# One block kernel on one core: the low half of every fourth weight unit of the SSD stage made by an accumulating load

## The chip, the cores and the metric

The kernel runs on one core of a Trainium2 chip. Its time is the device time of that core in microseconds (us): 2100.75 us, the median of 3 runs (2100.36 to 2102.08). Everything said of the inside of the kernel comes from one profiled execution, which took 2101.31 us; the profile's span, from the first to the last instruction, is 2099.6 us.

The engines are called by the profile's names: PE (matrix multiply) with PEld (its weight loads), DVE (VectorE), ACT (ScalarE), POOL (GpSimd) and SP (SyncE, which here only issues transfers).

## The reference

One residual block over 256 tokens of width 2048, in float32. The input is normalised (RMSNorm), multiplied by one large matrix, and its columns feed two token mixers: a stick-breaking attention of 16 heads, and a Mamba-2 SSD (64 heads of 64, 8 groups, chunks). Both are projected, gated, added, projected again and normalised; then a gated MLP with a short convolution follows. The part that the change touches is the projection into the SSD mixer and the mixer itself:

```python
proj = h @ w_in[i]
q, k, v, z, xbc, dt, g_sb, g_ssd = jnp.split(proj, cuts, axis=-1)
xbc = jax.nn.silu(causal_dwconv(xbc, ssd_conv_w[i], ssd_conv_b[i]))
xs, bm, cm = jnp.split(xbc, [SSD_INNER, SSD_INNER + SSD_GROUPS * SSD_STATE], axis=-1)
y = ssd_scan(xh, dt, a, bm, cm)
y = (y + xh * d_skip[i][:, None]).reshape(b, s, SSD_INNER) * jax.nn.silu(z)
y = rms_norm(y.reshape(b, s, SSD_GROUPS, SSD_INNER // SSD_GROUPS), ...)
```

Every product with a weight matrix has to come out with more than the precision of one pass of the matrix engine in its fast format (`fp32r`).

## The kernel before, in words

**Units.** All weights are cut on the host into 714 units of 128 x 1024 float32 (512 KB), in the order in which PE uses them. Each unit goes through three steps. SP loads it into `raw` (`load`, L74 to L79). ACT casts it to `fp32r` into `whi`, the high half (L63). DVE subtracts, `wlo = raw - whi`, which gives the low half (L64). L63 and L64 stand in the helper `split`, which `prep` calls (L81 to L95). PE then multiplies with both halves. `raw` has 5 buffers (`RBUFS`) and `whi` and `wlo` have 5 each (`WBUFS`).

**How far ahead.** `unit()` (L97 to L104) gives out the next unit's halves, and before that runs `prep` up to the unit three further on. With five buffers, the cast of unit v can start when PE has finished unit v - 5.

**Products.** `feat_mm` (L115, lines L112 and L113) makes 128 output features for all 256 tokens. It uses two units, and from each unit eight blocks of 128 x 128 as the stationary operand, first of `whi`, then of `wlo`. `tok_mm` (L136, lines L145 to L147) makes 512 features for 128 tokens at a time. It uses eight units for 2048 rows, and there the weights are the moving operand; each unit takes 12 matmuls.

**The SSD stage.** After eight joint units (0 to 7), the loop over the 8 groups uses units 8 to 161. A group is 4 feature tiles `ps_xs` (8 units), one `ps_bc` for B and one for C (2 units each), then `ps_z` (8 units): 20 units. The first group has only 14, since three of its `ps_xs` tiles come from the joint units. I number the units of a group 0 to 19: `ps_xs` has 0 to 7, `ps_bc` 8 to 11, `ps_z` 12 to 19.

**The work between.** The group's scan, `ssd_work` (L324 to L382), is a generator; `pump()` (L155) runs its next piece inside `ps_z` and the following `ps_xs`, after every fourth k step of `tok_mm` and after each feature tile. Its pieces follow each other through the engines: PE transposes the features (L332), DVE makes `xw` (L333) and `mm` (L338), POOL does three multiplications (L335, L336) and two masks (L339), ACT takes the exponential of `mm` (L347) and copies `pcb` (L345), then PE makes `po` (L353). Later DVE writes `csb` (L357), POOL adds it (L358), and PE makes `pd` (L363). POOL also issues two loads for each group: `csb<-gain` (L356, 256 KB) and the next group's `csb<-cs_dram` (L429, 1 MB).

**Order.** Each engine executes its own instructions in a fixed order. This order is not the order of the source: a planner in the framework writes it, and takes at each point an instruction whose operands are ready by its own reckoning, earlier source first. Across engines, semaphores enforce the dependencies. An instruction that waits holds up what stands behind it on the same engine, and this is so for transfers that POOL or SP issue as well. In the first part of the kernel and in two short stretches (`manual_schedule`), ACT and DVE keep the source's order.

Of the kernel before, what the change touches and what calls it, by code (L numbers as in the profile page):

```python
# [12 lines left out]
AF = mybir.ActivationFunctionType  # L13
ALU = mybir.AluOpType
# [18 lines left out]
ACT_DVE = {mybir.EngineType.Activation, mybir.EngineType.DVE}  # L33
WBUFS = 5
RBUFS = 5


@with_exitstack
def block_kernel(ctx, tc, xT, xN, wts, vecs, rows, hvec, dskip, gain, out):


    nc = tc.nc
    n_units = wts.shape[0]

    const = ctx.enter_context(tc.tile_pool(name="const", bufs=1))
    wraw = ctx.enter_context(tc.tile_pool(name="wraw", bufs=RBUFS))
    wspl = ctx.enter_context(tc.tile_pool(name="wspl", bufs=WBUFS))
# [14 lines left out]
    def split(hi, lo, src):  # L62
        nc.scalar.copy(hi, src)  # L63
        nc.vector.tensor_tensor(lo, src, hi.bitcast(F32), op=ALU.subtract)  # L64
# [9 lines left out]
    def load(u, parts=1):  # L74
        raw = wraw.tile([P, 1024], F32, tag="raw", name=f"raw{u}")
        n = 1024 // parts
        for i in range(parts):
            nc.sync.dma_start(raw[:, i * n:(i + 1) * n], wts[u][:, i * n:(i + 1) * n])
        raw_t[u] = raw  # L79

    def prep(parts=1):  # L81

        v = state["u"]
        state["u"] += 1
        if v not in raw_t:
            load(v)
        raw = raw_t.pop(v)
        hi = wspl.tile([P, 1024], F32R, tag="whi", name=f"whi{v}")
        lo = wspl.tile([P, 1024], F32R, tag="wlo", name=f"wlo{v}")
        spl_t[v] = (hi, lo)  # L90
        n = 1024 // parts
        for i in range(parts):
            w = slice(i * n, (i + 1) * n)
            split(hi[:, w], lo[:, w], raw[:, w])
            yield  # L95

    def unit(ahead=WBUFS - 2):  # L97

        u = state["at"]
        state["at"] += 1  # L100
        while state["u"] <= min(u + ahead, n_units - 1):
            for _ in prep():
                pass
        return spl_t.pop(u)  # L104
# [79 lines left out]
    for c in range(1, 4):  # L184
        nc.sync.dma_start(x_raw[c], xT[:, 4 * c:4 * c + 4, :])
        for u in range(2 * c, min(2 * c + 2, RBUFS)):
            load(u)

    with tc.manual_schedule(engines=ACT_DVE):
        lnexp()  # L190
        for c in range(4):
            ac = act_chunk(f"a{c}")
            steps = prep(2 if c == 0 else 1)
            for j in range(4):
                g = gpre[:, 4 * c + j:4 * c + j + 1]
                nc.scalar.activation(ac[:, j, 0, :], x_raw[c][:, j, :], AF.Copy, scale=g)
                nc.vector.scalar_tensor_tensor(ac[:, j, 1, :], x_raw[c][:, j, :], g, ac[:, j, 0, :].bitcast(F32), op0=ALU.mult, op1=ALU.subtract)
                if j == 3 or c == 0 and j == 1:
                    next(steps)
            for _ in prep():  # L200
                pass
            a_ch.append(ac)
# [606 lines left out]
```

## Time and profile before

| what | value |
|---|---|
| median of the runs | 2100.75 us (2100.36 to 2102.08) |
| the profiled execution | 2101.31 us, span 2099.6 us |
| PE busy | 2072.1 us, 99% of the span |
| DVE busy | 1386.0 us, 66% |
| ACT busy | 1156.9 us, 55% |
| POOL busy | 152.3 us, 7% |
| HBM read over the span | 396.71 MB |

The profile's page gives busy times, groups of instructions by line, the chain of waits that ended last, and the transfers. The trace behind it also answers for a stretch of the span. In a timeline row, the first two numbers are the start and the duration in us; rows of equal form that follow each other are merged (`x4`), and what stands in brackets is the idle time before, with the instruction that ended it. In a row of waits, the numbers are the total in us, how many times, and the longest. In a row of a group, the numbers after the bar are the busy us, the mean ns of one, and the idle us before them. The SSD stage lies between about 34 and 522 us, and its groups repeat every 62.9 us.

### The profile page before, as it was taken

What the parts mean: (1) busy time and instruction counts of PE and PEld (TensorE: products, weight loads), DVE (VectorE), ACT (ScalarE), POOL (GpSimd) and SP (SyncE); (2) the same over time, 40 slices, a digit from 0 to 9 for tenths busy, and PEclk for the clock granted to TensorE, in tenths of its full rate; (3) what the DMA queues carried; (4) which work ended last, traced back from release to release, by engine and by line L of the source; (5) the groups of instructions that cost most, each with busy time, mean ns of one, the idle gap of its engine ahead of it and who ended that gap; (6) DMA issues with size and microseconds to landing.
All of it is one profiled execution on the core that took longest, in us unless ns stands there. A gap on an engine that the chain in (4) does not pass through costs nothing.

```text
span 2099.6 us, 27950 instructions
## 1 busy us (share of the span) xinstructions
PE 2072.1 (99%) x10632; PEld 1760.7 (84%) x10632; DVE 1386.0 (66%) x1794; ACT 1156.9 (55%) x1542; POOL 152.3 (7%) x134
## 2 busy tenths in 40 slices
PE   9999999999999999999999999999999999999997
PEld 7788888888888888888888888788888888888886
DVE  6888877788544445555544566598878887854443
ACT  6767677667543334555556444475555555544442
POOL 0222102222000000000000021100000000000000
PEclk9999999999999999999999999999999999999999
DMA  8564565555555555555555746475555555565653
GB/s 297 194 205 160 190 205 186 176 199 179 187 197 192 192 194 186 180 171 171 170 172 185 274 161 210 141 250 191 189 190 190 189 189 190 191 232 202 195 193 109
DMA packets 109094, 402.79 MB, mean 192 GB/s; under 512 B 12416, under 2 KB 12672, under 8 KB 106656
## 3 DMA queue, kind: packets, MB, share of 16 engines
q1 hardware_dynamic: 104912, 380.07, 54.1%
q0 software_dynamic: 3328, 20.02, 2.7%
q8 instruction: 83, 1.36, 0.3%
q10 hardware_dynamic: 720, 0.93, 0.1%
q14 instruction: 51, 0.42, 0.1%
HBM read 396.71 MB, written 4.26 MB: 191 GB/s over the span
## 4 chain that ended last, share of the span: by engine, by line
PE 92%; POOL 2%; DVE 2%; issue 2%; DMA 1%; ACT 1%; SPq 0%; DVEq 0%; ACTq 0%; POOLq 0%
PE ps_fv L112 8%; PE ps_fg L112 8%; PE ps_qk L112 6%; PE ps_xs L112 5%; PE ps_fo L147 4%; PE ps_fo L145 4%; PE ps_fo L146 4%; PE ps_fg L113 4%; PE ps_fv L113 4%; PE ps_qk L113 3%; PE ps_ssd L147 3%; PE ps_ssd L145 3%; PE ps_ssd L146 3%; PE ps_xs L113 2%; PE ps_bc L112 2%; PE ps_z L146 2%
## 5 line engine op out<-in xcount | busy, mean ns | idle before, releaser
L64 DVE TENSOR_TENSOR wlo<-raw,whi 128x1024 fp32r<-128x1024 f32 (+1 forms) x715 | 905.1, 1270 | 601.2 <-ACT whi L63 600.6
L63 ACT CAST whi<-raw 128x1024 fp32r<-128x1024 f32 (+1 forms) x715 | 746.2, 1051 | 793.7 <-PE ps_fo L147 128.9
L112 PE MATMUL ps_fg<-h,whi 128*128 128x512 f32 x688 | 240.7, 394 | 0.0
L112 PE MATMUL ps_fv<-h,whi 128*128 128x512 f32 x688 | 240.6, 394 | 0.0
L113 PE MATMUL ps_fg<-h,wlo 128*128 128x256 f32 x688 | 190.6, 277 | 0.0
L113 PE MATMUL ps_fv<-h,wlo 128*128 128x256 f32 x688 | 190.6, 277 | 0.0
L112 PE MATMUL ps_qk<-a,whi 128*128 128x512 f32 x512 | 181.3, 398 | 0.0
L112 PE MATMUL ps_xs<-a,whi 128*128 128x512 f32 x464 | 162.9, 396 | 0.0
L112 PEld LDWEIGHTS ps_fv<-h,whi 128*128 128x128 f32 x688 | 129.0, 188 | 30.0
L112 PEld LDWEIGHTS ps_fg<-h,whi 128*128 128x128 f32 x688 | 129.0, 188 | 30.0
L113 PE MATMUL ps_qk<-a,wlo 128*128 128x256 f32 x512 | 143.5, 280 | 0.0
L145 PE MATMUL ps_fo<-whi,f 128*128 128x512 f32 x352 | 136.9, 389 | 0.0
L147 PE MATMUL ps_fo<-whi,f 128*128 128x512 f32 x352 | 136.9, 389 | 0.0
L146 PE MATMUL ps_fo<-wlo,f 128*128 128x512 f32 x352 | 136.9, 389 | 0.0
L113 PEld LDWEIGHTS ps_fg<-h,wlo 128*128 128x128 f32 x688 | 129.2, 188 | 0.0
L113 PEld LDWEIGHTS ps_fv<-h,wlo 128*128 128x128 f32 x688 | 129.2, 188 | 0.0
L113 PE MATMUL ps_xs<-a,wlo 128*128 128x256 f32 x464 | 129.0, 278 | 0.0
L112 PEld LDWEIGHTS ps_qk<-a,whi 128*128 128x128 f32 x512 | 96.1, 188 | 22.6
L145 PE MATMUL ps_z<-whi,a 128*128 128x512 f32 x256 | 103.7, 407 | 0.0
L112 PEld LDWEIGHTS ps_xs<-a,whi 128*128 128x128 f32 x464 | 87.1, 188 | 19.6
L146 PE MATMUL ps_z<-wlo,a 128*128 128x512 f32 x256 | 100.4, 392 | 1.0 <-DVE wlo L64 1.0
L147 PE MATMUL ps_z<-whi,a 128*128 128x512 f32 x256 | 100.1, 391 | 0.0
(282 smaller groups left out, 3832.5 us busy)
## 6 DMA issues: line engine op xcount, KB each, us to landing
raw<-wts SPq DMA_DIRECT2D x713, 512.0 KB, 3.8
csb<-cs_dram POOLq DMA_DIRECT2D x8, 1024.0 KB, 8.1
xt<-xN SPq DMA_DIRECT2D x2, 1024.0 KB, 10.6
csb<-gain POOLq DMA_DIRECT2D x8, 256.0 KB, 4.1
xn<-xN POOLq DMA_DIRECT2D x2, 1024.0 KB, 7.9
x_dram<-xn POOLq DMA_DIRECT2D x2, 1024.0 KB, 9.0
xe<-x_dram POOLq DMA_DIRECT2D x2, 1024.0 KB, 10.3
x<-xT SPq DMA_DIRECT2D x3, 512.0 KB, 9.2
```

The lines of the kernel that those rows point to most:

```text
L63: nc.scalar.copy(hi, src)
L64: nc.vector.tensor_tensor(lo, src, hi.bitcast(F32), op=ALU.subtract)
L112: nc.tensor.matmul(ps, hi[:, w], act[:, k % 4, :, :].rearrange("p s t -> p (s t)"), start=(k == 0), stop=last)
L113: nc.tensor.matmul(ps[:, :T], lo[:, w], act[:, k % 4, 0, :], start=False, stop=last, skip_group_check=True)
L145: nc.tensor.matmul(pss[t], ah, hi[:, w], start=(k == 0), stop=False)
L146: nc.tensor.matmul(pss[t], ah, lo[:, w], start=False, stop=False)
L147: nc.tensor.matmul(pss[t], al, hi[:, w], start=False, stop=(k == nk - 1))
```

## The change

`prep` gets a branch for units 12 to 161 whose number leaves 3 when divided by 4; these are 37 units (15, 19, ..., 159). For them ACT first writes the negated, rounded weights into `lo`. Then POOL issues a load of the same unit from HBM that adds to what is in `lo`. Then ACT writes `hi` as before. DVE takes no part. In a group these are the units that I number 1, 5, 9, 13 and 17. `raw` is still loaded for them, since both ACT instructions read it.

```diff
+SSD_U0, SSD_U1 = 12, 162
...
         hi = wspl.tile([P, 1024], F32R, tag="whi", name=f"whi{v}")
         lo = wspl.tile([P, 1024], F32R, tag="wlo", name=f"wlo{v}")
         spl_t[v] = (hi, lo)
+        if SSD_U0 <= v < SSD_U1 and v % 4 == 3:
+            nc.scalar.activation(lo, raw, AF.Copy, scale=-1.0)
+            nc.gpsimd.dma_start(out=lo, in_=wts[v], accum_op=ALU.add)
+            nc.scalar.copy(hi, raw)
+            return
         n = 1024 // parts
```

## The prediction

> **What bounds the kernel now.** I read the page first, then the table of stretches over the SSD stage, then PE's own waits in it.
>
> ```profile
> span 2099.6 us, 27950 instructions
> PE 2072.1 (99%) x10632; PEld 1760.7 (84%) x10632; DVE 1386.0 (66%) x1794; ACT 1156.9 (55%) x1542; POOL 152.3 (7%) x134
> ```
>
> ```profile
> core 0: us, PE busy (x) PEld busy (x) DVE busy (x) ACT busy (x) POOL busy (x), PEclk, DMA share, GB/s
> ...
> 60.00:110.00 50.00, 47.49 (x267) 39.70 (x266) 40.99 (x60) 35.34 (x50) 12.78 (x10) 1.00 0.65 226
> 110.00:470.00 360.00, 356.82 (x1955) 305.21 (x1954) 294.21 (x391) 252.53 (x338) 73.39 (x48) 1.00 0.56 187
> ```
>
> ```profile
> PE po L353 <- ACT xw L345: 3.7, 6, 0.7
> PE po L353 <- POOL xw L336: 2.4, 1, 2.4
> PE ps_z L146 <- DVE wlo L64: 1.0, 1, 1.0
> ```
>
> In the long middle of the stage, PE is busy for 356.8 of 360 us at a granted clock of 1.00. DVE is at 294 of 360 (82%), ACT at 252 (70%), POOL at 73 (20%). PE's waits between 20 and 540 us come to 3.7 + 2.4 + 1.0 = 7.1 us, and only 1.0 us of them is for a low half. So DVE, which the change relieves, isn't what the stage waits for. Whatever the change frees, it can't give back more than about 7 us of 2101, which is 0.34%. A loss has no such limit: a low half that comes late stops PE, which executes in order. The question is therefore whether the new way of making it is in time.
>
> **What goes and what comes.** The groups by line, between 130 and 480 us:
>
> ```profile
> L64 DVE TENSOR_TENSOR wlo<-raw,whi 128x1024 fp32r<-128x1024 f32 x110 | 149.2, 1373 | 21.5 <-ACT whi L63 21.5
> L63 ACT CAST whi<-raw 128x1024 fp32r<-128x1024 f32 x109 | 111.2, 1050 | 43.4 <-PE ps_z L147 14.8 <-PE ps_xs L112 14.6 <-PE ps_bc L112 10.2
> raw<-wts SPq DMA_DIRECT2D x110, 512.0 KB, 4.2
> csb<-cs_dram POOLq DMA_DIRECT2D x6, 1024.0 KB, 8.1
> csb<-gain POOLq DMA_DIRECT2D x6, 256.0 KB, 4.1
> ```
>
> DVE loses 37 subtractions of 1.37 us, 51 us in all. ACT gains 37 instructions of the form of a cast, at 1.05 us: 39 us, five in each group of 62.9 us, so that its 70% becomes about 78%. POOL gains 37 issues of some 0.6 us. SP's loads all stay. The transfers gain 37 x 0.5 MB = 19 MB; beside the stage's mean rate of 187 GB/s that is 5 x 0.52 MB in 62.9 us or some 42 GB/s more, which the DMA share of 0.56 leaves room for (0.13 more, or 0.25 if each adding byte counts twice).
>
> **ACT's extra cast: nothing.** It stands in front of casts with a margin. The worst place is the burst at 228.57, where the cast of unit 8 comes first, then the two of unit 9, then 10:
>
> ```profile
> 228.57 1.98 ACT L63 CAST whi<-raw 128x1024 fp32r<-128x1024 f32 x2
> 229.75 1.22 DVE L64 TENSOR_TENSOR wlo<-raw,whi 128x1024 fp32r<-128x1024 f32 x1
> 234.74 0.19 PEld L112 LDWEIGHTS ps_bc<-a,whi 128*128 128x128 f32 x1
> 237.62 0.19 PEld L113 LDWEIGHTS ps_bc<-a,wlo 128*128 128x128 f32 x1
> ```
>
> Unit 8's low half is ready at 229.75 + 1.22 = 230.97 and PE takes up the unit at 234.74: 3.8 us to spare, the smallest margin of an ordinary unit in the group. It isn't behind the extra instruction; unit 10, which is, comes 2.8 us later on PE. An added 1.05 us is covered. If this cover were gone, it would cost at most 1.05 us in each of 7 groups, 7 us.
>
> **The low half itself: the term that decides.** Before, it was ready 1.05 + 1.22 us after its cast began. Now it takes the negation (1.05), the issue on POOL and the landing. The time allowed runs from the end of the negation, which takes the place of the old cast, to PE's first weight load from `wlo`. For unit 9 the negation ends where the second cast did, at 228.57 + 1.98 = 230.55, and PE wants it at 237.62: 7.1 us. For unit 1:
>
> ```profile
> 202.96 3.90 ACT L63 CAST whi<-raw 128x1024 fp32r<-128x1024 f32 x4
> 212.77 0.19 PEld L113 LDWEIGHTS ps_xs<-a,wlo 128*128 128x128 f32 x1
> 174.90 1.05 ACT L63 CAST whi<-raw 128x1024 fp32r<-128x1024 f32 x1 [0.63 <-ACT y L63]
> 185.84 0.19 PEld L146 LDWEIGHTS ps_z<-wlo,a 128*128 128x128 f32 x1
> ```
>
> The four casts are those of units 0 to 3, so the second ends at 202.96 + 0.95 + 1.05 = 204.96, and PE wants unit 1 at 212.77: 7.8 us. Unit 13, the next tightest, has 185.84 - 175.95 = 9.9 us; units 5 and 17 have more. (Units 1 and 9 of the second group, at the stage's start, have about a microsecond more than in the six later groups, so I count six.)
>
> No row shows an adding load. The nearest are POOL's own: 4.1 us from issue to landing for 256 KB, 8.1 us for 1 MB. By size alone, 512 KB lies at 4.1 + (256/768) x 4.0 = 5.4 us. If the transfer has to read the destination as well as the source, it moves as much as the 1 MB load: 8.1 us. A bound below is 4.1, and one above is the longest of the 1 MB rows, 10.7 us:
>
> ```profile
> DMA to landing us min/median/max: 3.8/5.7/10.7
> ```
>
> I take the middle of 5.4 and 8.1, 6.8 us: the size stands halfway, and I have no row that says whether the second read is hidden behind the first. At 6.8 us both units are in time, by 0.3 and 1.0 us. This term is 0, with little margin.
>
> **The queue on POOL.** The issue waits for ACT, and everything behind it on POOL waits too. Behind unit 17's stands the scan's `xw`, behind unit 1's stands L358:
>
> ```profile
> 186.04 1.05 ACT L63 CAST whi<-raw 128x1024 fp32r<-128x1024 f32 x1 [0.76 <-PE ps_z L147]
> 190.48 1.03 POOL L336 TENSOR_TENSOR xw<-xw,dec 128x512 f32<-128x512 f32 x1 [43.58 <-DVE xw L333]
> 199.50 0.60 POOL L356 DMA_DIRECT2D csb<-gain  x1
> 207.16 2.10 POOL L358 TENSOR_TENSOR xs<-xs,csb 128x512 f32<-128x512 f32 x1 [7.06 <-DVE csb L357]
> ```
>
> Unit 17's issue is over at 187.09 + 0.60 = 187.7, before 190.48; unit 1's at 205.6, before 207.16. POOL then holds nobody up: 0. If POOL's mask came 0.6 us later after all, the wait for `po` below would grow by that, 4 us over the stage.
>
> **What may be gained.** `po` makes PE wait 0.6 us in each of six groups. The chain to it starts on DVE:
>
> ```profile
> 187.13 1.23 DVE L64 TENSOR_TENSOR wlo<-raw,whi 128x1024 fp32r<-128x1024 f32 x1 [0.69 <-ACT whi L63]
> 188.27 1.52 DVE L317 SCALAR_TENSOR_TENSOR cva<-cvr,vec,cva 128x255 f32<-128x255 f32 x3
> 189.70 1.28 DVE L333 TENSOR_TENSOR xw<-px,dt_tok 128x512 f32<-128x512 f32 x2
> ```
>
> The subtraction at 187.13 is unit 17's, and it goes. The three convolution steps and `xw` can then move up, until their own operands are late: ACT's and PE's, which aren't far ahead. So of the 0.6 us I take half, between 0 and all: 6 x 0.3 = 1.8 us (0 to 3.7). The 2.4 and 1.0 us in the first group hang on a chain of DVE, ACT and POOL that gets one relief and one load more; I take 0 for them.
>
> **Sum.** On the profiled execution, 2101.31 + 0 + 0 + 0 - 1.8 = 2099.5 us. It lies 0.6 us above the median of the runs, so against those it would be 2098.9. I forecast 2099.5: no change, since 0.2% (4.2 us) is about what a measurement of this kernel can tell from none.
>
> **The rivals.**
>
> *The adding load lands at 8.1 us or later: slower.* At 8.1, unit 9 is late by 1.0 and unit 1 by 0.3 us, 6 x 1.3 = 7.8, less 1.8: 2107.3 us. At 10.7, they are late by 3.6 and 2.9 and unit 13 by 0.8: 6 x 7.3 = 43.8, which gives 2143. The time passes the 0.2% when the load takes over about 8.0 us. For it: the second read, and the weight loads beside it, which slow the 1 MB rows as well. Against it: the 1 MB rows already hold twice the bytes written. The Trainium skill, in "Collectives: The Full Stack", section "The bandwidth ceiling: the fold count and why AG ≠ RS ≠ AR", says that an add in the transfer engine costs no cycles of its own but needs two source reads on the same ring, which halves the rate; by that rule the load behaves as the 1 MB one does, and the sum is this rival's 2107. No run here shows it yet. Chance 0.36.
>
> *Unit 1's load is queued behind L358: slower.* In the source, L356 to L358 come before unit 1's `prep`. If the planner keeps that order on POOL, the issue comes after 207.16 + 2.10 = 209.26 and lands at 216.1 with 6.8 us: 3.3 us late in six groups, 20 us, so 2119. It decides from a landing of 3.5 us on. Against it: on DVE, unit 1's subtraction stands ahead of L357, whose result L358 needs, so by the planner's reckoning the cast was ready first. Chance 0.08.
>
> *All of PE's waits go: faster.* 7.1 us at most: 2094.2. It needs the `po` wait gone in every group, and the first group's too. Chance 0.06.
>
> **How the numbers follow.** The forecast has 0.50; the three rivals have 0.36, 0.08 and 0.06. Faster by over 0.2% is the last alone, 0.06; slower is 0.36 + 0.08 = 0.44; the same is 0.50. The range begins at 2095.5, which is near all of the gain, and ends at 2125: that takes in the queue's 2119 and landings up to about 9.5 us (2.4 + 1.7 us late, 25 us), and leaves out the slower landings, some 0.13, and the last of the gain.
>
> **What would show it.** Right: the `lo` loads stand in the list of transfers with a landing of 6 to 7.5 us; PE's waits in the stage show no row that ends on the load of `lo`, and `po`'s wait is 1 to 3 us in place of 3.7; DVE's share of 110 to 470 falls from 82% to about 70%, ACT's rises to about 78%; the groups still repeat every 62.9 us. Wrong: PE waits for that load at unit 9, then at unit 1, in every group (the landing was mis-sized); or the load of unit 1 stands behind L358 on POOL (the queue was); or other casts come late (ACT's margin was).

## The result, and the profile after

The change made the kernel slower: 2153.0 us (median of 4 runs, 2151.59 to 2161.98) against 2101.41 us (4 runs of the kernel before on the same chip). The ratio is 1.0253, with a 95% interval of 1.024 to 1.0267. That is 51.6 us more, far outside the range. The profiled execution of after is the longest of its four runs: 2161.98 us, span 2160.3, so against the span of before (2099.6) it has 60.7 us to explain. In after's code the lines from L63 on are shifted: the cast is L65, the subtraction L66, the new negation L94, the adding load L95, the cast of a changed unit L96.

The page, with the busy times and the new transfers:

```profile
PE 2096.0 (97%) x10632; PEld 1776.9 (82%) x10632; DVE 1351.6 (63%) x1757; ACT 1184.9 (55%) x1577; POOL 177.0 (8%) x171
...
wlo<-wts POOLq DMA_DIRECT2D x37, 512.0 KB, 8.3
```

The 37 subtractions are gone (1794 to 1757 instructions on DVE), and 37 loads of 512 KB are there, with a median of 8.3 us to landing. The stretches of the stage, in the columns of before:

```profile
60.00:110.00 50.00, 43.29 (x207) 35.56 (x206) 29.12 (x42) 29.38 (x41) 13.05 (x12) 0.86 0.67 205
110.00:470.00 360.00, 334.50 (x1763) 283.86 (x1762) 237.55 (x331) 249.82 (x332) 79.41 (x66) 0.96 0.67 203
```

PE, which had been busy for 356.8 of 360 us, now is for 334.5, and the granted clock beside it, 1.00 before, is 0.96. Two things have come up, then: idle time, and time at a lower clock. The four largest of PE's waits between 20 and 600 us name the first:

```profile
PE ps_bc L120 <- DMA wlo<-wts: 25.0, 6, 4.7
PE ps_xs L120 <- DMA wlo<-wts: 9.5, 6, 2.2
PE pd L370 <- DVE mm L357: 3.5, 1, 3.5
PE ps_z L153 <- DMA wlo<-wts: 3.2, 1, 3.2
```

`ps_bc` is unit 9, at about 4.2 us in each of six groups; `ps_xs` is unit 1, at 1.6 us. The 3.7 us for `po` have gone. The `pd` row and the `ps_z` row are in the first group.

**Why unit 9 is late.** ACT's timeline in the second of the later groups (start, duration):

```profile
247.34 1.03 ACT L65 CAST whi<-raw 128x1024 fp32r<-128x1024 f32 x1
248.27 1.05 ACT L96 CAST whi<-raw 128x1024 fp32r<-128x1024 f32 x1
249.34 1.28 ACT L325 ACT_TABLE_LOAD   x1
250.63 0.42 ACT L325 ACTIVATE xf<-cva 128x256 f32<-128x256 f32 x1
250.96 0.35 ACT L140 COPY cvr<-ps_xs 128x256 f32<-128x256 f32 x1
251.21 1.06 ACT L94 ACTIVATE wlo<-raw 128x1024 fp32r<-128x1024 f32 x1
```

POOL's and PE's, around the same unit:

```profile
252.57 0.86 POOL L95 DMA_DIRECT2D wlo<-wts  x1 [19.45 <-ACT wlo L94]
```

```profile
256.66 0.39 PE L119 MATMUL ps_bc<-a,whi 128*128 128x512 f32 x1
261.28 0.58 PE L120 MATMUL ps_bc<-a,wlo 128*128 128x256 f32 x1 [4.23 <-DMA wlo<-wts]
```

At 247.34 is unit 8's cast. What follows it, in the place of the old cast of unit 9, isn't the negation but the cast to `whi` (L96). The source has the negation first, but the planner placed the cast ahead of it, and a table load of 1.28 us and two small instructions between the two. So the negation ends at 252.27, 4.9 us after unit 8's cast began, where the old cast ended 1.98 us after it. POOL issues 0.3 us later, and the load lands at 261.24, 8.67 us from its issue. PE had wanted it at 261.28 - 4.23 = 257.05. The time allowed was 4.8 us, and the load with its issue took 9.0. Unit 1 shows the same order with less between:

```profile
221.01 1.04 ACT L96 CAST whi<-raw 128x1024 fp32r<-128x1024 f32 x1
221.97 1.05 ACT L94 ACTIVATE wlo<-raw 128x1024 fp32r<-128x1024 f32 x1
```

```profile
231.61 0.38 PE L120 MATMUL ps_xs<-a,wlo 128*128 128x256 f32 x1 [1.36 <-DMA wlo<-wts]
```

The negation ends at 223.02, PE wants the unit at 231.61 - 1.36 = 230.25: 7.2 us allowed, 8.6 taken.

**The clock.** Two stretches of 4 us after unit 9's wait; the number before the last two is the granted clock:

```profile
262.00:266.00 4.00, 4.00 (x14) 3.32 (x13) 0.00 (x0) 0.00 (x0) 0.00 (x0) 0.50 1.04 363
268.00:272.00 4.00, 4.00 (x24) 3.48 (x23) 2.74 (x5) 1.55 (x2) 0.00 (x0) 1.00 0.76 251
```

PE is busy throughout in both, but finishes 14 matmuls in the first and 24 in the second. Each of the six waits of about 4 us at unit 9 had such a stretch behind it, and so had one wait at unit 1. PE's work in these seven stretches, from the end of the wait where the stretch began within it, at a granted clock of 0.50 or 0.51:

```profile
sum 32.00, PE 32.00 PEld 27.45 DVE 0.24 ACT 2.53 POOL 0.65; mean PE 4.57 PEld 3.92 DVE 0.03 ACT 0.36 POOL 0.09
```

At half the clock, half of these 32 us is lost, 16 us in all and 2.7 in each of the six groups, and no view of waits shows that loss. The Trainium skill, in "TensorE: Matmul & The Clock Gate", Part 1, says that the array falls to half rate after an idle window of about 3.4 us and comes back after as long a time of work; the trace agrees as to the halving and the time at half rate (3.4 or 6.8 us), but not as to the length of the idle time: the wait at unit 1 was 2.2 us.

**The sum.** The scan's `xw` on POOL stands once in a group, so its first and last start give the period; before, then after:

```profile
L336 POOL TENSOR_TENSOR xw<-xw,dec x3: 1033/1034/1036, 190.5 to 316.2; 128x512 f32<-128x512 f32 x3
```

```profile
L343 POOL TENSOR_TENSOR xw<-xw,dec x3: 1040/1040/1042, 207.6 to 351.0; 128x512 f32<-128x512 f32 x3
```

A group takes (351.0 - 207.6)/2 = 71.7 us where it took 62.85: 8.9 more. In the mean of all six later groups it is 8.5 more (71.4 us from `po` to `po`): 4.2 for unit 9, 1.6 for unit 1, -0.6 for `po` and 2.7 for the clock make 7.9. The other 0.6 us isn't placed. The first group, from its first `po` to the second group's, went from 61.3 us (77.6 to 138.9) to 68.5 (80.2 to 148.7), and what is ahead of it became 2.6 us longer. With 2.6 + 7.2 us there, the other 50.9 us are the six later groups at 8.5; what follows the stage takes as long as before.

### The profile page after: what moved, and what is told of

Its sections match the earlier page's. It is cut to its first block, busy times and chain, and to the rows that moved or that the text cites. A ratio compares the mean times of both kernels' runs of the same rounds, so it can differ in the third digit from the quotient of the medians.

```text
span 2160.3 us, 28005 instructions
## 1 busy us (share of the span) xinstructions
PE 2096.0 (97%) x10632; PEld 1776.9 (82%) x10632; DVE 1351.6 (63%) x1757; ACT 1184.9 (55%) x1577; POOL 177.0 (8%) x171
## 3 DMA queue, kind: packets, MB, share of 16 engines
q8 instruction: 83, 1.36, 0.3%
## 4 chain that ended last, share of the span: by engine, by line
PE 83%; DMA 6%; issue 4%; ACT 4%; DVE 2%; POOL 1%; SPq 0%; DVEq 0%; POOLq 0%
PE ps_fv L119 7%; PE ps_fg L119 7%; PE ps_qk L119 6%; DMA wlo<-wts 5%; PE ps_fo L153 4%; PE ps_fo L154 4%; PE ps_fo L152 4%; PE ps_fg L120 4%; PE ps_fv L120 4%; PE ps_qk L120 3%; PE ps_ssd L154 3%; PE ps_ssd L152 3%; PE ps_ssd L153 3%; PE ps_bc L119 2%; PE ps_xs L119 2%
## 5 line engine op out<-in xcount | busy, mean ns | idle before, releaser
L66 DVE TENSOR_TENSOR wlo<-raw,whi 128x1024 fp32r<-128x1024 f32 (+1 forms) x678 | 863.6, 1277 | 671.4 <-ACT whi L65 670.6
L65 ACT CAST whi<-raw 128x1024 fp32r<-128x1024 f32 (+1 forms) x678 | 709.1, 1049 | 829.4 <-PE ps_fo L154 129.3
L119 PE MATMUL ps_xs<-a,whi 128*128 128x512 f32 x464 | 168.1, 405 | 0.0
L152 PE MATMUL ps_z<-whi,a 128*128 128x512 f32 x256 | 104.4, 409 | 0.0
L120 PE MATMUL ps_bc<-a,wlo 128*128 128x256 f32 x256 | 78.4, 306 | 25.0 <-DMA wlo<-wts 25.0
```

The lines of the kernel that those rows point to most:

```text
L119: nc.tensor.matmul(ps, hi[:, w], act[:, k % 4, :, :].rearrange("p s t -> p (s t)"), start=(k == 0), stop=last)
L120: nc.tensor.matmul(ps[:, :T], lo[:, w], act[:, k % 4, 0, :], start=False, stop=last, skip_group_check=True)
L152: nc.tensor.matmul(pss[t], ah, hi[:, w], start=(k == 0), stop=False)
```

## The experiments

The theory: the adding load is late because it lands later than a plain one and because it begins later than I reckoned, and after a wait of about 4 us the clock adds to it. The rivals: that the extra work on ACT or the queue on POOL does it, that the transfers merely get in each other's way, or that units other than 9 and 1 do it. Each kernel is the changed kernel with the edit shown.

**1. The load left out.**

```diff
             nc.scalar.activation(lo, raw, AF.Copy, scale=-1.0)
-            nc.gpsimd.dma_start(out=lo, in_=wts[v], accum_op=ALU.add)
             nc.scalar.copy(hi, raw)
```

> The adding load is left out, so the low half of the 37 units is only the negated high half; both ACT instructions and the missing subtraction stay. If the loss is PE's wait for the adding load (theory A), PE has no such wait and the time is 2093 to 2101 us, a little under the kernel before since po's wait is gone. If the extra ACT instruction or the changed order of the casts costs the time (theory C), 2125 us or more stays.

Measured: 2104.52 us, ratio 1.0009 (0.9999 to 1.0018), some 3.5 us above the range of theory A and far below that of theory C. The longest of PE's waits between 20 and 600 us, and the middle stretch:

```profile
PE pd L369 <- DVE mm L356: 4.2, 1, 4.2
```

```profile
110.00:470.00 360.00, 359.23 (x1968) 307.25 (x1966) 262.26 (x363) 279.52 (x370) 67.97 (x47) 1.00 0.55 188
```

Without the load, ACT's extra instructions (279.5 of 360, 78%) cost the groups nothing: PE is busy for 359.2 of 360 us and `po` no longer waits. So the casts aren't the cause. The issue on POOL went with the load, so this run alone doesn't tell the queue from the landing; the rows of unit 9 above do, where the issue comes 0.3 us after the negation and 8.67 of the 9.0 us are the landing. What this kernel loses, it loses in the first group. The stretch from the first `po` to the first `pd`, before and here:

```profile
77.64:89.01 11.37, 11.25 (x55) 8.99 (x55) 6.37 (x6) 7.59 (x7) 6.39 (x5) 1.00 0.56 219
```

```profile
75.63:87.17 11.54, 7.34 (x32) 5.61 (x33) 7.79 (x7) 4.33 (x4) 6.73 (x5) 1.00 0.43 135
```

PE had about 55 matmuls there and now has 32: the planner has put `pd` more than 20 matmuls earlier in PE's order, where its operand `mm` isn't ready, so PE waits for 4.2 us. The changed kernel has a wait of 3.5 us at the same place.

**2 to 4. Which units.** The condition was narrowed to some of the five units of a group.

```diff
-        if SSD_U0 <= v < SSD_U1 and v % 4 == 3:
+        if SSD_U0 <= v < SSD_U1 and (v - 2) % 20 in (5, 13, 17):
```

> The adding load is made for units 5, 13 and 17 of each group alone (22 or 23 loads in place of 37), units 1 and 9 go through VectorE again. Theory A (units 1 and 9 are late, the others have 9.9 us or more): no wait of PE for a low half, 2094 to 2102 us. Rival B (the added transfers and POOL issues slow the stage as such, in proportion to their number): three fifths of the loss stay, about 2132 us.

Measured in experiment 2: 2109.93 us, 1.0039 (1.0028 to 1.005). The theory's number is missed, and the rival's by more.

```profile
PE ps_z L153 <- DMA wlo<-wts: 8.0, 5, 2.9
```

Unit 13 (`ps_z`), which I had counted as in time, is late too, in five groups, by up to 2.9 us. In the group where PE wants it at 192.42, the cast (L96) came first, at 181.09, and the negation ended at 184.66: 7.8 us were left of the 9.9.

> Of each group, unit 9 alone is made by the adding load (7 loads). Theory A: PE waits 3 to 4.5 us for each in six groups, and a stretch at half the granted clock follows each wait, which costs another 2 to 3 us: 2125 to 2142 us. If the half-speed stretches came from the added traffic and not from the wait, there would be none with so few loads: 2115 to 2125.

Measured in experiment 3, with `(9,)`: 2141.58 us, 1.0179 (1.016 to 1.0198).

```profile
PE ps_bc L120 <- DMA wlo<-wts: 25.8, 7, 4.9
PE po L360 <- ACT xw L352: 4.2, 7, 0.6
```

One load in each group makes 1.8 of the 2.5%; its waits are 25.8 us, and the clock and the first group are the rest. In the six later groups, five waits of 4.0 to 4.9 us had a half-clock stretch behind them, and one of 2.6 us had none. With a fifth of the loads the stretches are still there, so they come of the wait and not of the added traffic. With only one subtraction less per group, and not unit 17's, `po`'s wait stays.

> Of each group, unit 1 alone (7 loads). Theory A: PE waits 1 to 2.2 us for each in six groups, too short for the granted clock to fall: 2105 to 2113 us, and no half-speed stretch in the middle of the stage. If any wait brings the clock down, each costs 2 to 3 us more: 2120 or more.

Measured in experiment 4, with `(1,)`: 2117.01 us, 1.0062 (1.0045 to 1.008), between the two expected times. In the profiled execution, unit 1 is late by 7.3 us in six groups, with one half-clock stretch (3.4 us, after a wait of 2.1) that the theory had excluded, `po`'s wait is kept, and a `pd` wait of 7.1 us stands in the first group. The three kernels' losses add up to 2.8%, a little more than the change's 2.5%; each of them has a loss of its own in the first group.

**5. A plain load.** The low half is then the weights themselves.

```diff
-            nc.gpsimd.dma_start(out=lo, in_=wts[v], accum_op=ALU.add)
+            nc.gpsimd.dma_start(out=lo, in_=wts[v])
```

> The same 37 loads, without the addition: the low half is then the weights themselves, and the order of everything stays. Theory A with the doubled read as the cause of the landing: rows of 4096 bytes take about 160 ns again in place of 328, the load lands in 5 to 6 us, unit 9 is late by 0.6 to 1.6 us and unit 1 not at all, 2100 to 2113 us. Rival (the landing is long because the load shares the transfer engines with the weight stream): it stays near 8 us and the time near 2150.

Measured: 2109.88 us, 1.0029 (1.0017 to 1.004). The loads between 130 and 480 us, and PE's waits:

```profile
wlo<-wts POOLq DMA_DIRECT2D x28, 512.0 KB, 6.5
```

```profile
PE pd L370 <- DVE mm L357: 5.6, 1, 5.6
PE ps_bc L120 <- DMA wlo<-wts: 2.4, 5, 1.2
```

The landing is longer than the 5 to 6 us expected, the time is within the range. In the traces' packets, the rows of 4096 bytes on POOL's queue take 174 ns here (median) and 328 ns in the change. The bytes written and the order stay, and 43 of the 51.6 us go. Unit 9 is late by 1.2 us at most, too little for the clock to drop in the later groups.

**6. The negation first.** ACT's cast of a changed unit is held behind its negation, the order that the prediction had assumed.

```diff
-            nc.scalar.activation(lo, raw, AF.Copy, scale=-1.0)
+            neg = nc.scalar.activation(lo, raw, AF.Copy, scale=-1.0)
             nc.gpsimd.dma_start(out=lo, in_=wts[v], accum_op=ALU.add)
-            nc.scalar.copy(hi, raw)
+            with tc.issue_after(neg.ins):
+                nc.scalar.copy(hi, raw)
```

> The cast of the high half is held behind the negation on ACT for these units, nothing else. Theory A: the issue for unit 9 comes 1 to 3 us earlier, for unit 1 about 1 us earlier, so PE waits 1 to 3 us less in each group and the half-speed stretch is shorter or gone: 2110 to 2138 us. Rival (the order on ACT does not matter, since the load waits for something else): 2150 us.

Measured: 2118.46 us, 1.0075 (1.006 to 1.009).

```profile
PE pd L371 <- DVE mm L358: 5.5, 1, 5.5
PE ps_z L154 <- DMA wlo<-wts: 3.6, 1, 3.6
PE ps_bc L121 <- DMA wlo<-wts: 3.0, 3, 1.1
```

The order alone brings back 34.5 us. Unit 9 waits for 1.1 us at most, with a median landing of 8.0 us, and the clock stays at 1.00 in the later groups. The first two rows are the first group's. Experiments 5 and 6 give back 43 and 34.5 of 51.6 us, so they overlap: either one shortens unit 9's wait enough to spare the clock as well.

**7. Work in place of the wait.** Fourteen matmuls, whose result nobody reads, stand ahead of unit 9 in each group, just before the place where PE would wait.

```diff
+            if k == 8 and name.startswith("ps_bc") and name.endswith("_0"):
+                spare = mm_bank(f"warm_{name}")
+                for _ in range(14):
+                    nc.tensor.matmul(spare, acts[0][:, 0, 0, 0:P], acts[0][:, 0, :, :].rearrange("p s t -> p (s t)"), start=True, stop=True)
             feat_tile(ps, hi, lo, k % 8, acts[k // 4], k, k == KT - 1)
```

> The changed kernel with 14 matmuls of 512 columns, to a spare bank that nobody reads, put before unit 9's products in each group, about 3.2 us of work for PE where it waited 4.2 us. Theory A with the clock: PE's time in the wait is worth nothing anyway, the granted clock stays, and the half-speed stretches of 3.4 to 6.8 us go: 2153 falls by 12 to 24 us, to 2129 to 2141, although PE does 22 us more. If the clock has no part in it, the time stays at 2150 to 2160; if the wait was not what it seems, it rises by up to 22 us.

Measured: 2147.47 us, 1.021 (1.0188 to 1.0231), between the two expected numbers. Eleven of the spare matmuls of a group in one row, and PE's waits at units 1 and 9 between 20 and 600 us:

```profile
259.75 2.68 PE L130 MATMUL warm_ps_bc<-a 128*128 128x512 f32 x11
```

```profile
PE ps_xs L120 <- DMA wlo<-wts: 7.9, 6, 2.3
PE ps_bc L120 <- DMA wlo<-wts: 4.0, 3, 1.6
```

```profile
110.00:470.00 360.00, 349.87 (x1880) 296.89 (x1879) 245.05 (x344) 262.59 (x350) 80.58 (x67) 1.00 0.69 209
```

The granted clock in the middle is back at 1.00, with one short half-clock stretch left, after a wait at unit 1. Fourteen matmuls take 14 x 0.24 = 3.4 us, which fills most of the 4.2 us. If the wait alone mattered, the groups would be as long as in the change. From one group's first `po` to the next one's, they are 68.6 us in the mean of six, against 71.4: 2.8 us less. Some 0.4 of it is less time in waits and spare work together; the rest, 2.4 us, is the price of the half clock that has gone, near the 2.7 us above. In the first group this kernel lost 5.7 us more than the change did (74.2 against 68.5 us), so its time shows only part of it.

**8. More lead, from the second group on.** The negation and the load of a unit are made two units earlier in the program; units 12 to 41 are left as before the change. The edit is shown in part: the branch keeps only the cast, and the load into `raw` moves up with the negation.

```diff
-SSD_U0, SSD_U1 = 12, 162
+SSD_U0, SSD_U1 = 42, 162
...
+        e = v + 2
+        if SSD_U0 <= e < SSD_U1 and e % 4 == 3:
+            if e not in raw_t:
+                load(e)
+            lo_t[e] = wspl.tile([P, 1024], F32R, tag="wlo", name=f"wlo{e}")
+            nc.scalar.activation(lo_t[e], raw_t[e], AF.Copy, scale=-1.0)
+            nc.gpsimd.dma_start(out=lo_t[e], in_=wts[e], accum_op=ALU.add)
         raw = raw_t.pop(v)
```

> The negation and the adding load of a unit are written two units earlier, ahead of that unit's casts, with the low-half buffer taken then, and only from unit 42 on (30 units), so the first two groups stay as before. Theory A: 5.5 us more time for each load, no wait for a low half, no half-speed stretch, and po's wait of 0.6 us in each group is gone: 2095 to 2101 us. Rival B (the traffic itself, or ordinary units that now get their buffer later): 2106 us or more.

Measured: 2100.22 us, 0.9995 (0.998 to 1.0009): no difference. PE's waits between 20 and 600 us, all of them, then the groups' `xw`:

```profile
PE po L365 <- POOL xw L348: 2.4, 1, 2.4
PE ps_z L158 <- DVE wlo L66: 1.2, 1, 1.2
```

```profile
L348 POOL TENSOR_TENSOR xw<-xw,dec x3: 1041/1045/1045, 190.0 to 314.7; 128x512 f32<-128x512 f32 x3
```

Nothing waits for the load any more, so the added transfers as such cost nothing. `po`'s wait of the later groups has gone, and a group takes 62.35 us, 0.5 less than before the change. So this is all that DVE's relief is worth: some 3 us in six groups, about 0.15%.

**9. The change, from the second group on** (only the first line of the edit above).

> The changed kernel with units 12 to 41, the first group of chunks and what is ahead of it, left as they were before; changed from unit 42 on. Theory (the first group is lost to the planner's new order on TensorE, 32 matmuls in place of 54 between its first po and its first pd, and to units 15 to 39 being late): the way to the second group's first po, 138.9 us before and 148.7 after the change, is 139 again, so about 10 us of the 51.6 come back, 2141 to 2146. Rival (the first group's loss only moves on to the group that is the first changed one): 2149 to 2155, and the pd wait turns up in that group.

Measured: 2142.83 us, 1.0193 (1.0174 to 1.0212). The second group's first `po` is back at 139.6 us, as the theory said, and 10.2 us of the 51.6 have gone. That is the first group's share.

**10. More lead, the first group too.**

> Negation and adding load made two units earlier in the program, as in the kernel before this one, but for all the changed units, the first group's too. Theory (time between negation and use is all that the groups lack; the first group loses to the order): groups of 62.4 us, no half-clock stretch after 140 us, and in all 2100 to 2108, what it is above 2098 being the first group's. Rival (with enough lead the first group loses nothing either): 2094 to 2099, faster than before.

Measured: 2115.9 us (2107.69 to 2117.91), 1.0054 (1.0034 to 1.0073); more than the theory had. The groups are at 62.4 us and no half clock shows from 140 us to the end of the stage, as it said, but PE waits long at the first `po`:

```profile
PE po L365 <- POOL xw L348: 6.2, 1, 6.2
```

The reason stands on POOL, where `csb<-cs_dram` and then `xw` wait for the landing of the store `cs_dram<-dts`; before the change, then here:

```profile
71.73 0.57 POOL L429 DMA_DIRECT2D csb<-cs_dram  x1 [3.66 <-DMA cs_dram<-dts]
```

```profile
77.67 0.61 POOL L441 DMA_DIRECT2D csb<-cs_dram  x1 [8.44 <-DMA cs_dram<-dts]
```

The store is issued at 67.52 before the change and at 68.36 here, right behind an adding load; it lands after 4.2 us there and 9.3 here. By these rows the loads do hold up POOL's queue in the first group, though no low half is late.

By the end of the stage, this kernel is 4.5 us behind the kernel before the change, with the last group's first `po` at 520.6 against 516.1 us. Some 9 us more come up after 1400 us, in code that the edit doesn't touch. From 1420 to 1620 us PE is never idle and its clock is 1.00, as in experiment 8, and yet it finishes 1134 matmuls where it finished 1157 there, 2% fewer. Why stays open; single runs of experiment 8 itself reach from 2097.82 to 2109.33 us, so a difference of this size isn't shown to come of the edit.

**11. One unit of lead, from the second group on** (`e = v + 1`).

> Negation and adding load one unit earlier in the program, from unit 42 on. Theory: one unit is about 5.6 us of TensorE's time; unit 9 then has about 10 us for a landing of 8.7, so nothing is late by more than 1 us, the groups are 62.4 us, and the time is that of two units earlier, 2097 to 2101, no different from before by more than 0.2%. Rival (the planner eats the lead again, as it does in the change): waits of 1 to 4 us at unit 9 or 1, half-clock stretches, 2105 to 2125.

Measured: 2112.55 us, 1.0044 (1.003 to 1.0059). The time lies where the rival had it, but not by the rival's way: PE waits for no load, but for ACT.

```profile
PE po L365 <- ACT xw L357: 11.1, 6, 2.6
```

One unit of lead is enough for the load, but in the order that the planner makes of it, ACT reaches the scan's `xw` later, and `po`'s wait, 0.6 us in a group before, becomes 1.9. The three longest of these waits, 2.0 to 2.6 us, each had 3.4 us of half clock behind them.

**12. The plain load, where nothing is late**: experiment 8 with the load left plain.

> The kernel with negation and load two units earlier, from unit 42 on, with the load left plain: it writes the weights over the negated half in place of adding them to it, so the low half is the weights themselves. The instructions and their order stay, and nothing waits for the load in either, so the 28 loads between 130 and 480 us stand in the same traffic: 7.0 us median with the addition. Theory (the addition is what lengthens the landing): 5.0 to 6.0 us here, the issue 0.54 us in place of 0.86, and the same time, 2096 to 2101. Rival (the landing is set by the raw loads beside it, and the 6.5 against 8.3 us of the plain load in the changed kernel came of the waits): 6.6 to 7.2 us.

Measured: 2098.48 us (one run, on another chip than experiment 8's). The transfers between 130 and 480 us, in experiment 8 (adding) and then here (plain):

```profile
q0 software_dynamic: 5232, 21.50, 31.3%
...
raw<-wts SPq DMA_DIRECT2D x112, 512.0 KB, 5.3
wlo<-wts POOLq DMA_DIRECT2D x28, 512.0 KB, 7.0
```

```profile
q0 software_dynamic: 5232, 21.50, 20.0%
...
raw<-wts SPq DMA_DIRECT2D x112, 512.0 KB, 4.4
wlo<-wts POOLq DMA_DIRECT2D x28, 512.0 KB, 5.3
```

The same packets and bytes hold POOL's queue for 31.3% of the engines' time when they add, and for 20.0% when they don't. The landing is 7.0 against 5.3 us, and SP's raw loads beside them land 0.9 us later as well. The addition itself lengthens the transfer, as experiment 5 has it too (6.5 against 8.3 us); the rival falls.

## Why the prediction was wrong, point by point

- **DVE isn't the bound, a gain is at most 7 us, a loss has no such limit**: right. With everything in time (experiment 8) the whole gain is 3 us of the profile, which its runs can't tell from none.
- **ACT's extra cast costs nothing**: right for the later groups (experiment 1, 359.2 of 360 us busy), at the 78% that was forecast.
- **POOL's queue holds nobody up**: right for the change, though the issue took 0.86 us where 0.60 was taken. Unit 17's loads are out in time, and unit 1's issue came ahead of L365 (before, L358), so that rival didn't come about. In experiment 10, in another order, the loads did hold up POOL in the first group.
- **`po` gives 1.8 us, between 0 and 3.7**: the mechanism was right and the size near; 0.5 us came back in each group where 0.3 was taken, 3 us in all.
- **"The time allowed runs from the end of the negation, which takes the place of the old cast"**: this step failed. The planner put the cast to `whi` in that place, and the negation behind it and, for unit 9, a table load and two small instructions. Unit 9 had 4.8 us instead of 7.1, unit 1 7.2 instead of 7.8, and unit 13, given 9.9, was late as well once it stood alone with 5 and 17. The order alone is worth 34.5 us (experiment 6). The sum also left out the 0.3 us from the end of the negation to the issue, which by itself would have used up unit 9's margin of 0.3. The text quotes the source's order in the rival on L358 but doesn't ask what order the planner gives two new instructions that are free to change places.
- **The landing, 6.8 us as the middle of 5.4 and 8.1**: too low. It was 8.3 us in the change, 7.0 with nothing late, and 5.3 for the plain load there, which is the size interpolation. The addition isn't hidden, as the rival had it; that the second read is what it costs, no row shows. The Trainium skill's rule, in "Collectives: The Full Stack", section "The bandwidth ceiling: the fold count and why AG ≠ RS ≠ AR", that the add's two source reads halve the rate, agrees in direction: POOL's queue took 1.6 times as long over the same bytes, of which about two thirds were added, and a row of 4096 bytes 1.9 times as long (328 against 174 ns). By the rival's own working, 8.3 us would have given some 2110 (6 x (1.2 + 0.5) - 1.8 above 2101.3), not 2153. So this term alone isn't the miss.
- **The sum counted waits only**: a term was missing. A load that is late by about 4 us costs the wait and then about 2.7 us of work lost at half clock (experiment 7 has 2.4), some 16 us in six groups. Before the change, no wait in the stage was longer than 2.4 us and none had half clock behind it, but the same trace has a longer one further on, which the prediction didn't look at, so the bounds could have had this term. PE waits 2.9 us for DVE at 1350 us, and then its clock is 0.50, while no transfer runs:

```profile
1353.00 1.32 PE L385 MATMUL pth<-ident,mog 128*128 128x128 f32 x6 [2.91 <-DVE mog L632]
```

```profile
1353.60:1356.90 3.30, 3.27 (x16) 3.11 (x16) 3.30 (x6) 2.17 (x4) 0.00 (x0) 0.50 0.00 0
```

- **"I take 0" for the first group**: wrong. It is 10.2 us (experiment 9). Part of it is late loads, part the planner's moving `pd` forward (experiment 1, where there is no added load at all).

Taken one after the other: with the measured landing and the order assumed, the kernel stands at 2118.5 (experiment 6), 17 us above before, most of it the first group's; the order adds 34.5 to that, in waits of 4 us and the half clock behind them. Not settled: why the planner prefers the cast to the negation, what 0.6 us of each later group is, and why experiment 10 is slower in the part after the stage.

## What to carry to other kernels

When an instruction is replaced by two, don't assume that the first of them gets the old one's place: where a planner orders the engines, price the other order too, and the work that it then lets in between. A step on a path with a fixed deadline is worth its lead, not its length: the same transfer, two units earlier, cost nothing. And an engine at 99% has no use for relief elsewhere, while an operand that is late by some 3 us or more costs it twice, once in the wait and once in the clock behind it.

## What the runs showed of the hardware that was not expected

- In the SSD stage of these 14 traces, every wait of PE of 3.2 us or more had a stretch at a granted clock of 0.50 around its end or just behind it. Of the 16 waits of 2.0 to 2.9 us, ten had one. The same wait of 2.4 us at the first `po` had none before the change and in experiments 9 and 12, and had 3.4 us of it in experiments 8 and 11, so the length of the wait alone doesn't decide. The stretches came in pieces of 3.4 us: 3.4, 6.8 or 10.2.
- POOL's issue of an adding load takes 0.86 us, that of the same load without addition 0.54:

```profile
L95 POOL DMA_DIRECT2D wlo<-wts x25: 851/860/882, 134.6 to 477.4; - x25
```

```profile
L95 POOL DMA_DIRECT2D wlo<-wts x28: 537/540/580, 131.9 to 475.7; - x28
```

- An adding load slows its neighbours: with 28 of them, the 1 MB load of `csb` had a median landing of 10.1 us against 7.5 with the plain ones (experiments 8 and 12).
